# Two empty steps at the end of an mLSTM part: the next part begins two ticks later

## Chip, core and metric

One core of a Trainium2 chip runs the whole program. The metric is device time in microseconds (us), the median of several executions. A core has five instruction queues that run beside each other and wait for each other by semaphores: TensorE (PE; its weight loads are shown as PEld), VectorE (DVE), ScalarE (ACT), GpSimd (POOL) and SyncE (SP), which here issues the DMAs.

## What is computed

One layer of a hybrid decoder block on 2048 positions of width 1024, float32. The part that matters here, cut from the reference:

```python
mod = c_act @ w_ada[l] + b_ada[l]
sh1, sc1, gt1, sh2, sc2, gt2 = [m[:, None, :] for m in jnp.split(mod, 6, axis=-1)]
h = rms_norm(x, g_mix[l]) * (1.0 + sc1) + sh1
p = h @ w_in                      # q_a k_a v_a | q_m k_m v_m o_m | u_s v_s | gates
y_attn = forgetting_attention(qa, ka, va, fa)          # 8 heads of 64
hm = mlstm_chunkwise(qm, km, vm, im, fm)               # 4 heads of 64
y_mlstm = jax.nn.sigmoid(o_m) * rms_norm(hm, g_m_out)
y_sgu = spatial_gating(gelu(u_s), gelu(v_s), g_sgu, w_s, b_s)
x = x + gt1 * (jnp.concatenate([y_attn, y_mlstm, y_sgu], -1) @ w_out)
x = x + gt2 * conv_ffn(rms_norm(x, g_ffn[l]) * (1.0 + sc2) + sh2, ...)
```

The mLSTM carries a state from one chunk of positions to the next, so its chunks are done in order.

## The kernel before

The program has a projection stage (h @ w_in with the mLSTM, the spatial gating and the preparation of the attention's q, k and v), then attention, the output projection, and the feed-forward network. The change is in the projection stage.

Every large product is made of three passes on split operands (a high and a low part): `mm3`, lines 54 to 56. The positions are taken in two halves of 1024. For each half seven blocks of columns are projected, in the list `blocks`: km with the gates, q/o of the mLSTM, vm, the gating's u and v (`use_sgu`), then the attention's k, q and v. A block has eight products of 24 large matmuls (8 steps of k, three passes each); `products` runs one of them. The result of a product stands in one of three PSUM buffers `acc` until VectorE and ScalarE have read it.

From the second block of a half to its sixth, every engine's order is as written (`manual_schedule`), and it is made by ticks. `tick` is called at the end of each product, and in blocks of 512 columns also in the middle of it, after twelve large matmuls. A tick does three things: it may advance a chore by one step (`rest_of_mod`, the remaining modulation vectors, whose accumulation on VectorE, lines 480 to 488, is summed over partitions on PE two ticks later: line 502 for columns, copied out by lines 505 and 507, or line 496 for a gate row, copied out by line 498); it runs what `after(n, f)` has put off until now (`due`); and it advances the first generator in the list `background` by one step, to its next `yield`. Only when that generator has ended is it taken off the list, and the next one begins at the following tick.

The generators are `rows(qi)`, which prepares the gates, and `mlstm(qi)`, a part of 512 positions in four chunks of 128. `mlstm(0)` and `mlstm(1)` belong to the first half, `mlstm(2)` and `mlstm(3)` to the second; the second of each pair stands behind the first in `background`. A part does, in order: loads of two chunks (lines 962 to 970); three empty steps; `turned(0)`, the transposes of kn (line 978, copied to kT by ScalarE, line 980); `decay(0)` (matmuls 952 and 953, exponentials 956) with `turned(1)`; then for each chunk a step with the scores and the state's share (1001, 1003, read by VectorE in 1004, 1005), a step with the values and the state's update (1018, 1022, read in 1019, 1031; the load of the chunk after next is issued here), and a step with the next decay. At its end stands the normalisation of all four chunks (1044 to 1057, on VectorE, ScalarE and GpSimd), two empty steps, one more multiply (1060), and two transposes back, put off by several ticks by `after` (`leave`: 1066 on PE, 1068 on VectorE, 1069 the write).

Beside it, at their own ticks: line 750 mixes positions for the gating, 759 transposes its result (761 copies it on ScalarE); 783 to 791 normalise a product for k or q, and 799 transposes it one and a half products later (803 on ScalarE, 804 on VectorE, 806 the writes to k_d or q_d). `wr` (line 599) are the next block's weights, cast by lines 609 and 610.

Four PSUM names are shared. `mp` has one buffer: lines 502, 496 and 978 write it. `mps` has two: 952, 1001, 1003, 1018, 1022 and 1066 take them in turn. `trp` has two: 750, 759, 799.

Of the kernel before, what the change touches and what calls it, by code (L numbers as in the profile page):

```python
# [33 lines left out]
def trunk(  # L34
# [356 lines left out]
    def mps():  # L391
        return pp.tile([P, 512], F32, name="mps", tag="mps")
# [257 lines left out]
    def natural(half, wb, consume):  # L650
        wide[0] = wb.width == 512
        for i in range(8):
            tt = half * 8 + i
            tb, o = tt // 4, (tt % 4) * P
            ps = acc_ps()

            def mm(k):
                hh, hl = hT[tb, k]
                mm3(ps[:, : wb.width], hh[:, o : o + P], hl[:, o : o + P], *wb.tiles[k], k == 0, k == KT - 1)

            products(i, mm)
            consume(tt, ps)

    def after(n, f):

        pending.append((ticks[0] + n, f))
# [37 lines left out]
    def use_vm(tt, ps):  # L704
        t = pool.tile([P, 256], F32, name="ev", tag="ev")
        V.tensor_copy(t, ps[:, 0:256])
        dma(vm_d[tt * P : (tt + 1) * P, :], t)
        if tt % 8 == 3:
            background.append(mlstm(tt // 4))
# [230 lines left out]
    def mlstm(qi):  # L940
# [122 lines left out]
        def leave(j):  # L1063
            yp = mps()
            for n in range(4):
                T.transpose(yp[:, n * P : (n + 1) * P], hq2[:, n, j * P : (j + 1) * P], ident)
            yt = pool.tile([P, 512], F32, name="yt", tag=("ra", "rb")[j])
            V.scalar_tensor_tensor(yt, yp, gmo[:, j : j + 1], om[:, j, :], op0=ALU.mult, op1=ALU.mult)
            dma(yt_d[512 + j * P : 640 + j * P, t0 : t0 + 512], yt)

        for j in range(2):
            after(6 + j if qi % 2 == 0 else 4 + j, lambda j=j: leave(j))

    nat = lambda use: lambda h, w: natural(h, w, use)
    blocks = [
# [18 lines left out]
    for n, (half, i) in enumerate(steps):  # L1094
# [34 lines left out]
        if i == 2:  # L1129
            background.append(mlstm(half * 2 + 1))  # L1130
# [666 lines left out]
```

## Time and profile before

| | us |
|---|---|
| median of 3 runs | 2602.79 |
| the runs | 2603.23, 2602.79, 2601.43 |
| the profiled execution, its own time | 2602.01 |
| its span, first to last instruction | 2600.3 |

The mean granted clock of TensorE was 0.998 of full speed. mlstm(1) begins its loads at 208.8 us and sends its last write at 299.96; mlstm(3) sends its last at 631.93.

How to read the rows: a row of the time line gives the start in us, the duration in us, the engine, the line of the program, the operation, what it writes and reads, its size, how many instructions of the kind were merged, and in brackets how long the engine stood idle ahead of it and what ended that. A row of waits gives who waited for whom: us in total, times, longest. SPq and PEq are queues ahead of an engine. A row on a tile gives the durations in ns (least, median, most) and the first and last start in us.

### The profile page before, as it was taken

What the parts mean: (1) busy time and instruction counts of PE and PEld (TensorE: products, weight loads), DVE (VectorE), ACT (ScalarE), POOL (GpSimd) and SP (SyncE); (2) the same over time, 40 slices, a digit from 0 to 9 for tenths busy, and PEclk for the clock granted to TensorE, in tenths of its full rate; (3) what the DMA queues carried; (4) which work ended last, traced back from release to release, by engine and by line L of the source; (5) the groups of instructions that cost most, each with busy time, mean ns of one, the idle gap of its engine ahead of it and who ended that gap; (6) DMA issues with size and microseconds to landing.
All of it is one profiled execution on the core that took longest, in us unless ns stands there. A gap on an engine that the chain in (4) does not pass through costs nothing.

```text
span 2600.3 us, 36330 instructions
## 1 busy us (share of the span) xinstructions
PE 2531.4 (97%) x12521; PEld 2094.4 (81%) x12537; DVE 2010.0 (77%) x3433; ACT 1270.3 (49%) x2424; POOL 403.9 (16%) x529
## 2 busy tenths in 40 slices
PE   5999999999999999999999999999999999999999
PEld 5888888888777877778877888888888888788787
DVE  7657656476388888865679888888888887898797
ACT  4343343432388878844455444444444444444443
POOL 2013310133266556510000000000000000000000
PEclk9999999999999999999999999999999999999999
DMA  7345762455564445266823222255222218558523
GB/s 249 114 129 150 218 190 88 136 150 147 172 165 125 128 126 167 54 196 233 283 81 98 81 83 80 82 215 178 85 81 85 86 65 283 174 169 293 184 98 118
DMA packets 302593, 379.58 MB, mean 146 GB/s; under 512 B 31935, under 2 KB 194589, under 8 KB 300361
## 3 DMA queue, kind: packets, MB, share of 16 engines
q1 hardware_dynamic: 302408, 377.26, 46.1%
q8 instruction: 99, 1.62, 0.3%
q14 instruction: 86, 0.70, 0.1%
HBM read 276.44 MB, written 100.74 MB: 145 GB/s over the span
## 4 chain that ended last, share of the span: by engine, by line
PE 43%; DVE 4%; DMA 3%; ACT 1%; issue 0%; SPq 0%; POOL 0%; DVEq 0%; ACTq 0%
PE ub L56 10%; PE ub L54 10%; PE ub L55 10%; PE db L55 4%; PE db L56 4%; PE db L54 4%; DMA wd<-in_w_down_dram 1%; DVE wspl L1474 1%; DMA hc_d<-hl 1%; DMA x_d<-x 0%; DVE wspl L1343 0%; DMA act<-act_d 0%; DVE t2w L1454 0%; DVE B L1208 0%; ACT wsph L1342 0%
## 5 line engine op out<-in xcount | busy, mean ns | idle before, releaser
L54 PE MATMUL acc<-wh,hh 128*128 128x512 f32 (+2 forms) x768 | 284.2, 371 | 1.9 <-DVE vhl L777 1.2
L54 PE MATMUL ub<-T,wsph 128*128 128x512 f32 x704 | 275.9, 392 | 6.5 <-ACT wsph L1342 2.4
L55 PE MATMUL ub<-T,wsph 128*128 128x512 f32 x704 | 275.8, 392 | 0.9 <-DVE T L1208 0.7
L56 PE MATMUL ub<-T,wspl 128*128 128x512 f32 x704 | 275.2, 391 | 0.8 <-DVE wspl L1343 0.7
L56 PE MATMUL acc<-wh,hl 128*128 128x512 f32 (+2 forms) x768 | 273.8, 360 | 1.2 <-DVE st L535 0.9
L55 PE MATMUL acc<-wl,hh 128*128 128x512 f32 (+2 forms) x768 | 273.5, 358 | 0.7 <-DVE wl L610 0.7
L55 PE MATMUL db<-wspl,wsph 128*128 128x512 f32 x616 | 241.0, 392 | 4.9 <-DVE wspl L1474 4.8
L56 PE MATMUL db<-wsph,wspl 128*128 128x512 f32 x616 | 239.5, 389 | 0.0
L54 PE MATMUL db<-wsph 128*128 128x512 f32 x616 | 239.5, 389 | 0.0
L1342 ACT CAST wsph<-S 128x512 fp32r<-128x512 f32 x176 | 109.4, 622 | 217.9 <-PE ub L55 156.5
L263 DVE TENSOR_TENSOR plo<-tp,phi 128x512 fp32r<-128x512 f32 (+1 forms) x320 | 186.9, 607 | 31.0 <-ACT phi L262 28.9
L54 PE MATMUL ub<-B,wsph 128*128 128x512 f32 x528 | 205.7, 390 | 0.0
L55 PE MATMUL ub<-B,wsph 128*128 128x512 f32 x528 | 205.4, 389 | 0.0
L56 PE MATMUL ub<-B,wspl 128*128 128x512 f32 x528 | 205.3, 389 | 0.0
L223 ACT ACTIVATE L<-L,nm 128x1024 f32<-128x1024 f32 (+2 forms) x192 | 172.5, 902 | 34.6 <-DVE nm L212 32.8
L259 PE MATMUL tp<-ident,L 128*128 128x128 f32 x1088 | 177.6, 275 | 4.1 <-DVE plo L263 1.5
L262 ACT CAST phi<-tp 128x512 fp32r<-128x512 f32 (+1 forms) x320 | 160.0, 521 | 42.9 <-PE tp L259 41.2
L1473 ACT CAST wsph<-act 128x512 fp32r<-128x512 f32 x132 | 82.3, 623 | 195.1 <-PE db L55 175.7
L206 PE MATMUL sp<-kk,q 128*128 128x512 f32 (+3 forms) x640 | 170.4, 377 | 3.2 <-DVE nm L212 2.2
L228 POOL TENSOR_SCALAR L<-L,rs 128x1024 f32<-128x1024 f32 (+2 forms) x192 | 167.7, 883 | 11.0
L56 PEld LDWEIGHTS acc<-wh,hl 128*128 128x128 f32 x768 | 144.8, 190 | 23.2 <-DVE hl L580 1.9
L54 PEld LDWEIGHTS ub<-T,wsph 128*128 128x128 f32 x704 | 132.8, 189 | 37.4 <-ACT wsph L1342 6.5
(323 smaller groups left out, 5940.3 us busy)
## 6 DMA issues: line engine op xcount, KB each, us to landing
w<-in_w_up_dram SPq DMA_DIRECT2D x88, 512.0 KB
wd<-in_w_down_dram SPq DMA_DIRECT2D x176, 256.0 KB
wa<-in_w_ada_dram SPq DMA_DIRECT2D x96, 256.0 KB
act_d<-yc SPq DMA_DIRECT2D x44, 512.0 KB
act<-act_d SPq DMA_DIRECT2D x44, 512.0 KB
wr<-in_w_in_dram SPq DMA_DIRECT2D x64, 256.0 KB
q<-q_d SPq DMA_DIRECT2D x128, 128.0 KB
hc_d<-hl SPq DMA_DIRECT2D x28, 512.0 KB
```

The costliest lines, as they stand in the source:

```text
L54: T.matmul(ps, lh, rh, start=start, stop=False, skip_group_check=resume)
L55: T.matmul(ps, lh, rl, start=False, stop=False, skip_group_check=resume)
L56: T.matmul(ps, ll, rh, start=False, stop=stop, skip_group_check=resume)
L206: T.matmul(sp[:, b : b + bw], q2[n][:, qs], kk[:, s0 + b : s0 + b + bw], start=n == 0, stop=n == 1 and not last)
L223: A.activation(L[c], L[c], AF.Exp, bias=nm[:, n - 1 : n], scale=-1.0, accum_out=rs[:, c : c + 1])
L228: G.tensor_scalar(t, t, rs[:, 0:1], 1.0, op0=ALU.mult, op1=ALU.mult)
L259: T.transpose(tp[:, i * P : (i + 1) * P], rows[i][j // 8][:, (j % 8) * P : (j % 8 + 1) * P], ident)
L262: A.copy(hi[:, c0:], tp[:, c0:])
L263: V.tensor_tensor(lo[:, c0:], tp[:, c0:], hi[:, c0:].bitcast(F32), op=ALU.subtract)
L1342: A.copy(hi, src)
L1473: A.copy(hi, v)
L1474: V.tensor_tensor(lo, v, hi.bitcast(F32), op=ALU.subtract)
```

## The change

At the end of the generator `mlstm` two empty steps are added, after `leave` has been put off:

```diff
         for j in range(2):
             after(6 + j if qi % 2 == 0 else 4 + j, lambda j=j: leave(j))
+        yield
+        yield
 
     nat = lambda use: lambda h, w: natural(h, w, use)
```

A part that has done its work stays in `background` for two more ticks, so the part behind it begins two ticks later. What `after` has put off keeps its tick; the chores and the products keep theirs. Behind mlstm(1) and mlstm(3) nothing waits in the list when they end. Outside the stretches of mlstm(1) and mlstm(3) the order of every engine is the same as before, and each engine has the same instructions.

The order moves in three places that are spoken of below. First, TensorE in the gating block of the first half, where the modulation sum (502) writes mp. Before, the transposes of kn (978) for mlstm(1) follow it:

```order
L56 MATMUL acc<-wh,hl 128x512
L502 MATMUL mp<-ones,modacc 128x1 x4
L978 MATMUL mp<-ident,kn 128x128 x2
L54 MATMUL acc<-wh,hh 128x512
L55 MATMUL acc<-wl,hh 128x512
```

Now they stand two ticks further on, behind a leaving transpose of mlstm(0) and a mixing product:

```order
L56 MATMUL acc<-wh,hl 128x512
L1066 MATMUL mps<-ident,hq 128x128 x4
L750 MATMUL trp<-sv,wT 128x256 x2
L978 MATMUL mp<-ident,kn 128x128 x2
L54 MATMUL acc<-wh,hh 128x512
```

Between 502 and 978 there are now 24 large matmuls, two mixing products and one group of leaving transposes.

Second, VectorE at the end of mlstm(1), where the sum of a modulation vector (482, 488) for the next 502 is made. Before:

```order
L1055 TENSOR_REDUCE mss<-hq 128x16
L1056 TENSOR_SCALAR mss<-mss 128x16
L785 TENSOR_REDUCE ss<-qsq 128x8
L786 TENSOR_SCALAR ss<-ss 128x8
L482 SCALAR_TENSOR_TENSOR modacc<-wa,cs,modacc 128x512
L791 TENSOR_TENSOR qn<-acc,ss 128x512
L804 SCALAR_TENSOR_TENSOR qlo<-trp,colA,qhi 128x512
L1060 TENSOR_TENSOR hq<-H,mss 128x1024
L785 TENSOR_REDUCE ss<-qsq 128x8
L786 TENSOR_SCALAR ss<-ss 128x8
L482 SCALAR_TENSOR_TENSOR modacc<-wa,cs,modacc 128x512
L488 TENSOR_TENSOR modacc<-modacc,brow 1x512
```

Now:

```order
L1055 TENSOR_REDUCE mss<-hq 128x16
L1056 TENSOR_SCALAR mss<-mss 128x16
L785 TENSOR_REDUCE ss<-qsq 128x8
L786 TENSOR_SCALAR ss<-ss 128x8
L482 SCALAR_TENSOR_TENSOR modacc<-wa,cs,modacc 128x512
L488 TENSOR_TENSOR modacc<-modacc,brow 1x512
L791 TENSOR_TENSOR qn<-acc,ss 128x512
L804 SCALAR_TENSOR_TENSOR qlo<-trp,colA,qhi 128x512
L1060 TENSOR_TENSOR hq<-H,mss 128x1024
```

The normalisation has come one product closer to 488, which now stands ahead of the multiply qn (791) and of 1060.

Third, TensorE in the second half, where the gate row (496) writes mp. Before, it stands ahead of a decay:

```order
L56 MATMUL acc<-wh,hl 128x512
L759 MATMUL trp<-ident,sy 128x128 x4
L496 MATMUL mp<-modacc,ones 128x512
L952 LDWEIGHTS selb
L952 MATMUL mps<-neb_290,selb 128x128
```

Now:

```order
L56 MATMUL acc<-wh,hl 128x512
L759 MATMUL trp<-ident,sy 128x128 x4
L496 MATMUL mp<-modacc,ones 128x512
L1001 MATMUL mps<-qz_295,kT 128x256 x2
L1003 MATMUL mps<-Cst,qT 128x130 x2
```

The gate row keeps its tick, and the part's first scores (1001, 1003) have come to it; the transposes of the second kn (978) for chunk 1 stand twelve large matmuls ahead of it.

## The prediction

> **What bounds the kernel now.** I read the page's first part, then a table of stretches, then who makes TensorE wait in the two stretches that the change touches.
>
> ```profile
> span 2600.3 us, 36330 instructions
> PE 2531.4 (97%) x12521; PEld 2094.4 (81%) x12537; DVE 2010.0 (77%) x3433; ACT 1270.3 (49%) x2424; POOL 403.9 (16%) x529
> 80.00:120.00 40.00, 40.00 (x187) 33.10 (x187) 28.08 (x52) 11.44 (x22) 0.00 (x0) 1.00 0.36 103
> 216.10:219.60 3.50, 1.22 (x10) 1.06 (x10) 2.16 (x8) 0.00 (x0) 1.54 (x2) 1.00 0.94 298
> ```
>
> TensorE (PE) is busy 97% of the span. The third and fourth rows are stretches: length, then busy time of PE, PEld, DVE, ACT and POOL, granted clock, DMA share and GB/s. From 80 to 120 us PE has no gap at all; from 216.10 to 219.60 it works 1.22 us of 3.50. So PE's own work sets the time, and what another order can change is only the gaps. Those gaps, by what ended them (total us, times, longest), in the first half's stretch from 190 to 320 us (four rows) and the second half's from 540 to 660 (three rows):
>
> ```profile
> PE mp L978 <- DVE sh L505: 2.3, 1, 2.3
> PE mp L502 <- DVE modacc L488: 0.5, 1, 0.5
> PE acc L55 <- DVE wl L610: 0.3, 1, 0.3
> PE trp L799 <- DVE qn L791: 0.2, 1, 0.2
> ...
> PE mps L1003 <- DVE yt L1068: 0.4, 1, 0.4
> PE acc L55 <- DVE wl L610: 0.4, 1, 0.4
> PE trp L799 <- DVE qn L791: 0.2, 1, 0.2
> ```
>
> All of them together are 4.3 us. That is the most this change could win here, and one wait is more than half of it.
>
> The Trainium skill, "Perfetto Trace Analysis", section "Identifying the Most-Contended Engine", says that matmul busy time is not a good measure for TensorE and that weight-load busy time should be used. By it the 81% of PEld would leave a fifth of the span as headroom, in which 2.3 us could vanish: that would be a time of about 2602.8. The trace differs: in the stretch without any gap PEld stands at 33.10 of 40 us, 83%, so 81% is already nearly all that this mix of instructions can show.
>
> **The change part by part.** It adds no instruction on a compute engine. mlstm(0) and mlstm(2) stay in the background queue for two ticks longer, so the whole of mlstm(1) and mlstm(3), with its loads, comes two ticks later. A tick here is half a product: twelve matmuls, from 219.70 to 222.54, 2.84 us; so the parts move by some 5.7 us of PE work.
>
> *The large wait.* Rows of the time line:
>
> ```profile
> 216.17 1.05 PE L502 MATMUL mp<-ones,modacc 128*128 128x1 f32 x8
> 217.76 0.43 DVE L737 TENSOR_TENSOR sv<-ev,mu 128x256 f32<-128x256 f32 x1 [1.12 <-POOL mu L128]
> 218.11 0.68 DVE L785 TENSOR_REDUCE ss<-qsq 128x8 f32<-128x512 f32 x1
> 219.30 0.15 DVE L505 COPY sh<-mp 128x4 f32<-128x4 f32 x1
> 219.50 0.44 PE L978 MATMUL mp<-ident,kn 128*128 128x128 f32 x2 [2.29 <-DVE sh L505]
> 219.70 0.48 PE L54 MATMUL acc<-wh,hh 128*128 128x512 f32 x1
> 222.31 0.39 PE L56 MATMUL acc<-wh,hl 128*128 128x512 f32 x1
> 222.54 1.02 PE L750 MATMUL trp<-sv,wT 128*128 128x256 f32 x4
> ```
>
> The modulation sum (L502) writes the one buffer mp; VectorE empties it (L505) only after what stands ahead in its queue, which itself waited for GpSimd; the transposes of kn (L978) want the same buffer and follow at once. In PE's queue nothing may pass them, so the twelve products behind stand still too. In the new order 24 large matmuls (about 5.7 us) and three small groups lie between the two, while L505 was ready 3.1 us after L502 began (219.30 against 216.17). The wait is gone: 2.29 us. Is something late next? VectorE's L505 no longer releases anyone soon; the next mixing products (L750 at 222.54) come 2.3 us earlier and need sv, written by 218.2. They fit.
>
> *The end of a part.* The normalisation of mlstm(1) now falls one product later, directly ahead of the next modulation sum:
>
> ```profile
> 274.35 0.60 PE L799 MATMUL trp<-ident,qn 128*128 128x128 f32 x4
> 276.38 0.17 DVE L1044 TENSOR_SCALAR nd<-H 128x16 f32<-128x16 f32 x1
> 280.28 0.60 PE L799 MATMUL trp<-ident,qn 128*128 128x128 f32 x4
> 280.98 0.68 DVE L785 TENSOR_REDUCE ss<-qsq 128x8 f32<-128x512 f32 x1
> 281.77 0.75 DVE L482 SCALAR_TENSOR_TENSOR modacc<-wa,cs,modacc 128x512 f32<-128x512 f32 x1
> 285.68 0.69 DVE L791 TENSOR_TENSOR qn<-acc,ss 128x512 f32<-128x512 f32 x1 [3.16 <-POOL ss L128]
> 289.65 0.68 DVE L488 TENSOR_TENSOR modacc<-modacc,brow 1x512 f32<-1x512 f32 x1
> 290.38 1.05 PE L502 MATMUL mp<-ones,modacc 128*128 128x1 f32 x8 [0.47 <-DVE modacc L488]
> ```
>
> Before, the sum (L488) stood behind qn, which waited 3.16 us for GpSimd, and PE then waited 0.47. Now L488 stands ahead of that qn. On the old clock: the chain began 2.03 us after the transposes at 274.35 and would begin 2.03 after those at 280.28, at 282.31. From its start to L785 were 4.60 us, to L482 another 0.79, then 0.75 and 0.68: L488 ends at 289.13. PE wants it at 290.38 less 0.47, 289.91. The margin is 0.78, so the wait goes: 0.47 us. If the chain ran 0.78 late, nothing would be won here, and every further us is a loss. The small wait of L799 on qn (0.2) I let stand: its cause, the chain ahead of qn, only moves.
>
> *Second half.* Two terms:
>
> ```profile
> 558.98 0.71 PE L1003 MATMUL mps<-Cst,qT 128*128 128x130 f32 x4 [0.38 <-DVE yt L1068]
> ...
> 482.29 0.44 PE L978 MATMUL mp<-ident,kn 128*128 128x128 f32 x2 [1.14 <-ACT kT L980]
> ...
> 220.37 1.28 ACT L956 ACT_TABLE_LOAD   x1
> 224.04 1.14 ACT L956 ACTIVATE M<-mps,acol 128x128 f32<-128x128 f32 x4 [2.38 <-PE trp L750]
> 225.05 0.39 ACT L980 COPY kT<-mp 128x256 f32<-128x256 f32 x1
> 232.61 0.60 PE L799 MATMUL trp<-ident,qn 128*128 128x128 f32 x4
> 233.25 0.69 ACT L803 ACTIVATE qhi<-trp,colA 128x512 fp32r<-128x512 f32 x1 [7.31 <-PE trp L799]
> ```
>
> L1003 waited 0.38 us because the leaving transposes of mlstm(2) held one of the two mps buffers; they now come a whole half product ahead of the next user of that buffer: 0.38 won. A new neighbour: the gate product L496, which also writes mp, now follows the transposes of kn by only twelve matmuls. With E as the product's end: leaving transposes 0.43 (232.18 to 232.61), L799 0.44 (to 233.05), the decay matmuls 0.44, kn's transposes 0.38, twelve matmuls 2.84, L759 0.44 make L496 wanted at E+4.97. ScalarE starts qhi 0.64 after L799, at E+1.07, and then needs 0.69, table 1.28, M 1.14 and kT 0.39: E+4.57. It fits by 0.4 us. Bounds: 0, and 1.14, the one wait of this kind (L978 behind kT at 482.29). I take 0.2, near the lower end, since the sum fits.
>
> *The DMAs.* Each part's twenty loads (kn, qT, two qz and v for four chunks) sit on SP's queue and move too. mlstm(1)'s third load now stands behind two k_d writes that wait for ScalarE and VectorE:
>
> ```profile
> L962 SPq DMA_DIRECT2D kn<-km_d x16: 326/469/974, 136.5 to 575.7; - x16
> L1010 POOL TENSOR_TENSOR kw<-kn,ecol x16: 607/611/615, 139.5 to 595.5; 128x256 f32<-128x256 f32 x16
> SPq L762 <- ACT evq L761: 8.7, 2, 7.3
> 241.24 0.60 PE L799 MATMUL trp<-ident,qn 128*128 128x128 f32 x4
> 244.43 0.97 SPq L962 DMA_DIRECT2D kn<-km_d  x1
> ```
>
> Behind such writes kn was issued 3.2 us after L799 (241.24 to 244.43), and the first kn landed within 3.0 us (136.5 to the multiply that waited for it at 139.5). In the new order L799 of the next product runs at E+9.55 (E+4.97, then 1.3 for L1001 and L1003, 2.84, 0.44), so kn is there at E+15.75. Its transposes come at E+19.36 (0.44 more, 1.45 for L1018 and L1022, 2.84, the decay 0.45, 2.84, L799 0.44, 1.35). Cover 3.6 us: it costs nothing, and beyond that PE stalls us for us. The x loads that reuse tiles of a part slip by a product as well; they are needed only in the next half's first block.
>
> **Sum.** 2.29 + 0.47 + 0.38 - 0.2 = 2.94 us less. The profiled execution took 2602.01 us (span 2600.3 and 1.7 around it), so 2599.07. The median of the three runs is 2602.79, 0.78 above it: predicted 2599.9.
>
> **The rivals.**
> 1. *Absorbed*: PE arrives 2.3 us earlier at a wait that was hidden, in the k block or later; VectorE is busy 77% of the span. For: all seven waits above are for VectorE. Against: VectorE stood idle itself in the rows above (1.12 and 3.16 us, for GpSimd), so it can follow an earlier PE. Time 2602.8, up to 2603.9 with the full 1.14.
> 2. *Slower*: SP's queue is held before the third load of a part. A write there has waited 7.3 us (L762 row). Held so long, kn is late by 7.3 less the cover of 3.6, 3.7 us, in both halves 7.4; less 2.94 it is 4.5 us more: 2607.3. It turns to a loss when the hold exceeds 3.6 + 1.5 us. Against: the writes ahead of this load wait for copies that ScalarE starts 0.64 us after the transposes.
> 3. *More*: every gap of both stretches closes, 4.3 us: 2598.5, and with the run to run spread (2601.43 to 2603.23) 2597.6.
> 4. *Not what it says*: the two ticks fall where the queue is empty. Against: the order of PE's queue does move, at exactly the wait. 2602.8.
>
> **How the numbers follow.** Forecast 0.64, absorbed 0.18, slower 0.08, more 0.07, nothing 0.03. The likeliest by itself spans 2598.5 to 2601.3. The range takes in 'more' and 'absorbed': 2597.5 to 2603.9. A change of 0.2% is 5.2 us, about what a measurement of this kernel can tell from none: faster means below 2597.6, slower above 2608.0. The forecast's own spread barely reaches the first; from 'more' I take 0.08 for faster, from 'slower' 0.05, and 0.87 remains.
>
> **What would show it.** Right: no row of L978 waiting for L505; PE without a gap between L502 and L750 near 216; no wait of L502 on L488 near 288; no wait of L1003 on L1068; the rest of the kernel starting some 2.5 to 3 us earlier. Wrong: L496 or L978 waiting for kT or for kn, L502's wait grown, or gaps of PE elsewhere that grew by what was won.

## The result and the profile after

| | before | after |
|---|---|---|
| median, us | 2602.82 | 2596.41 |
| lowest and highest run | 2600.35, 2607.48 | 2594.83, 2602.30 |
| the profiled execution | 2602.01 | 2596.29 |
| its span | 2600.3 | 2594.6 |

The ratio of after to before is 0.9979, 95% interval [0.9972, 0.9986]: 5.5 us less, between 3.6 and 7.3. (The two medians of the table differ by 6.4, inside that interval; what is compared from here on is the ratio with its interval.) The sign and the places were as predicted, the size was not: 2.9 us had been forecast, and 2596.4 lies 1.1 us below the low end of the range.

The first part of the page after: span, then busy time of each engine.

```profile
span 2594.6 us, 36323 instructions
PE 2530.4 (98%) x12521; PEld 2095.3 (81%) x12537; DVE 2010.4 (77%) x3433; ACT 1270.5 (49%) x2424; POOL 403.0 (16%) x529
```

PE's busy time is 2531.4 before and 2530.4 now, with the same number of matmuls; the span fell by 5.7. The work did not shrink. Who makes PE wait in the changed kernel, first in the stretch from 190 to 320 us, then from 535 to 660:

```profile
PE acc L55 <- DVE wl L610: 0.3, 1, 0.3
...
PE acc L55 <- DVE wl L610: 0.4, 1, 0.4
```

These two rows are all that is left of seven in this profile. The time line of the changed kernel, PE where the large gap was, PE at the next modulation sum, and VectorE ahead of that sum:

```profile
216.48 1.05 PE L502 MATMUL mp<-ones,modacc 128*128 128x1 f32 x8
217.39 0.48 PE L54 MATMUL acc<-wh,hh 128*128 128x512 f32 x1
...
220.23 1.02 PE L750 MATMUL trp<-sv,wT 128*128 128x256 f32 x4
...
223.86 0.60 PE L1066 MATMUL mps<-ident,hq 128*128 128x128 f32 x4
224.29 1.03 PE L750 MATMUL trp<-sv,wT 128*128 128x256 f32 x4
225.16 0.38 PE L978 MATMUL mp<-ident,kn 128*128 128x128 f32 x2
...
287.15 0.39 PE L56 MATMUL acc<-wh,hl 128*128 128x512 f32 x1
287.38 0.95 PE L502 MATMUL mp<-ones,modacc 128*128 128x1 f32 x8
...
280.28 0.17 DVE L1044 TENSOR_SCALAR nd<-H 128x16 f32<-128x16 f32 x1
284.88 0.68 DVE L785 TENSOR_REDUCE ss<-qsq 128x8 f32<-128x512 f32 x1
286.45 0.68 DVE L488 TENSOR_TENSOR modacc<-modacc,brow 1x512 f32<-1x512 f32 x1
```

The products follow L502 after 0.91 us (216.48 to 217.39) where they took 3.53 before, and L978 stands 8.7 us behind L502, with no idle time ahead of it. L488 ends at 287.13 and L502 starts at 287.38, 0.23 behind the last product, the distance of one product from the next.

A measure of the first half follows from two rows, the first transposes of the gating's result (L759) and the first transposes of the second half's normalised x (L574). They stand outside the moved part, and the work of PE between them is the same in both orders. A measure of the second half is made in the same way, from its own first L759 to the first matmul of the attention (L206):

```profile
203.93 0.60 PE L759 MATMUL trp<-ident,sy 128*128 128x128 f32 x4
...
367.51 1.03 PE L574 MATMUL trp<-ident,xt 128*128 128x128 f32 x8
...
532.89 0.60 PE L759 MATMUL trp<-ident,sy 128*128 128x128 f32 x4
...
666.51 0.62 PE L206 MATMUL sp<-kk,q 128*128 128x512 f32 x2
```

For the kernel before, the same four rows:

```profile
203.59 0.60 PE L759 MATMUL trp<-ident,sy 128*128 128x128 f32 x4
...
370.56 1.03 PE L574 MATMUL trp<-ident,xt 128*128 128x128 f32 x8
...
536.48 0.60 PE L759 MATMUL trp<-ident,sy 128*128 128x128 f32 x4
...
670.89 0.61 PE L206 MATMUL sp<-kk,q 128*128 128x512 f32 x2
```

The first half takes 163.6 us after and 167.0 before: 3.4 won, where the forecast had 2.76. The second takes 133.6 after and 134.4 before: 0.8 won, where the forecast had 0.18. These lengths, "the first half" and "the second half" from here on, are the finest rulers in the case. The total is a coarse one: executions of the same program spread over some 8 us.

### The profile page after: what moved, and what is told of

The parts are those of the page before. It is cut to its first block, busy times and chain, and to the rows that moved or that the text cites. A ratio compares the mean times of both kernels' runs of the same rounds, so it can differ in the third digit from the quotient of the medians.

```text
span 2594.6 us, 36323 instructions
## 1 busy us (share of the span) xinstructions
PE 2530.4 (98%) x12521; PEld 2095.3 (81%) x12537; DVE 2010.4 (77%) x3433; ACT 1270.5 (49%) x2424; POOL 403.0 (16%) x529
## 4 chain that ended last, share of the span: by engine, by line
PE 43%; DVE 4%; DMA 3%; ACT 1%; issue 0%; SPq 0%; POOL 0%; DVEq 0%; ACTq 0%
PE ub L56 10%; PE ub L55 10%; PE ub L54 10%; PE db L55 4%; PE db L56 4%; PE db L54 4%; DMA wd<-in_w_down_dram 2%; DVE wspl L1476 1%; DMA hc_d<-hl 1%; DMA x_d<-x 0%; DVE wspl L1345 0%; DMA act<-act_d 0%; DVE t2w L1456 0%; DVE B L1210 0%; DVE T L1210 0%
## 5 line engine op out<-in xcount | busy, mean ns | idle before, releaser
L55 PE MATMUL ub<-T,wsph 128*128 128x512 f32 x704 | 275.8, 392 | 0.9 <-DVE T L1210 0.7
L55 PE MATMUL acc<-wl,hh 128*128 128x512 f32 (+2 forms) x768 | 274.1, 359 | 0.7 <-DVE wl L610 0.7
L55 PE MATMUL db<-wspl,wsph 128*128 128x512 f32 x616 | 241.1, 392 | 5.3 <-DVE wspl L1476 5.0
L55 PE MATMUL ub<-B,wsph 128*128 128x512 f32 x528 | 205.4, 389 | 0.0
L206 PE MATMUL sp<-kk,q 128*128 128x512 f32 (+3 forms) x640 | 169.4, 375 | 3.3 <-DVE nm L212 2.2
L228 POOL TENSOR_SCALAR L<-L,rs 128x1024 f32<-128x1024 f32 (+2 forms) x192 | 167.7, 883 | 11.0
```

What stands on the lines that cost most here:

```text
L55: T.matmul(ps, lh, rl, start=False, stop=False, skip_group_check=resume)
L206: T.matmul(sp[:, b : b + bw], q2[n][:, qs], kk[:, s0 + b : s0 + b + bw], start=n == 0, stop=n == 1 and not last)
L228: G.tensor_scalar(t, t, rs[:, 0:1], 1.0, op0=ALU.mult, op1=ALU.mult)
```

## The experiments

The letters in an expectation are those of its own text. From the fifth run on they are: A, a closed gap is worth its own length; G, the gap of 2.29 us also lowers PE's granted clock behind it.

| run | median us | ratio to before, 95% interval | first half us | clock below 1 at 216 to 224 us |
|---|---|---|---|---|
| profile of before | 2602.82 | 1 | 167.0 | no |
| after | 2596.41 | 0.9979 [0.9972, 0.9986] | 163.6 | no |
| e1_control | 2602.04 | 1.0003 [0.9994, 1.0012] | 168.4 | yes |
| e2_first | 2596.72 | 0.9982 [0.9973, 0.9990] | 163.6 | no |
| e3_second | 2599.84 | 0.9997 [0.9988, 1.0006] | 168.4 | yes |
| e4_both | 2595.11 | 0.9979 [0.9970, 0.9988] | 163.6 | no |
| e5_mp | 2597.22 | 0.9984 [0.9975, 0.9992] | 164.5 | no |
| e6_fill | 2603.60 | 1.0009 [1.0000, 1.0018] | 167.1 | no |
| e7_one | 2596.56 | 0.9980 [0.9971, 0.9989] | 163.5 | no |
| e8_putback | 2600.72 | 0.9998 [0.9989, 1.0007] | 167.7 | yes |
| e9_fill2 | 2603.27 | 1.0006 [0.9996, 1.0015] | 167.0 | no |
| e10_backfill | 2599.15 | 0.9992 [0.9983, 1.0000] | 166.2 | no |
| e11_fill_next | 2599.30 | 0.9990 [0.9981, 0.9999] | 163.6 | no |
| e12 to e15, single runs | 2602.59, 2598.50, 2595.54, 2604.33 | | 168.3, 167.1, 167.1, 168.6 | yes, no, no, yes |

Each row's before is that of its own chip session.

### One half at a time

The empty steps stand under a condition. In e2_first it is `qi == 0`, in e3_second `qi == 2`, and e4_both has none, which is the change itself. For the control, e1_control, it is the one below: the steps stand where the list is empty anyway, so that its order is that of before (the edit against before):

```diff
+        if qi % 2 == 1:
+            yield
+            yield
```

> The two empty steps stand only at the end of mlstm(1) and mlstm(3), behind which nothing waits: every engine's instructions and order are those of the kernel before. All theories: the time of before, ratio 1.000. What it tells is how far two executions of one program differ, and whether the wait of 1.14 us of L978 on kT near 482 us, seen in the one profile of before, is there each time (theory A: it hangs on when a w_in transfer lands and comes and goes; theory B: it belongs to the old order and will be there again).

> The two empty steps only after mlstm(0), so only mlstm(1) begins later. Theory A (the sum of the closed TensorE gaps): 2.29 + 0.47 + 0.15 = 2.9 us less, 2599.9. Theory C (an earlier TensorE also wins later, in attention and in the output projection, about as much again): 4.5 to 6 us less.

> The two empty steps only after mlstm(2), so only mlstm(3) begins later. Theory A: 0.38 + 0.16 = 0.5 us less, 2602.3. Theory B (the 1.14 near 482 us is closed by the change in the first half): no more than 0.5 here either. If the whole change gives 6 us and the first half alone 3, then this must give 2 to 3, and the closed gaps are not the account.

> The changed kernel once more, on the same chip as the halves: 5.5 to 6.4 us less than before if the first result stands; 3 us if it was the chip. The halves should add up to it (theory A: 2.9 + 0.5 = 3.4).

Most of the gain lies in the first half: 0.9982 there, 0.9997 in the second, and both together 0.9979, which is their product. By the total the second half cannot be told from nothing; its ruler tells it: 134.36 to 134.43 us in each of the ten profiles with the old order there, 133.46 to 133.65 in each of the seven with mlstm(3) moved. Theory C for the first half (4.5 to 6 us) is not told from A (2.9) by the interval of 2.6 to 7.0. But no later gain shows where C looked for it: from the first L206 to the feed-forward network's first product it is 636.8 to 641.0 us in the seven profiles with the old first half, and 637.8 to 640.5 in those of after, e2, e4 and e7. The rows of waits went where the parts of the edit were: the first half's edit left L1003's 0.4, the second's left L978's 2.3.

The control has the program of before, and its total is not told from that of before, but its time line behind the gap reads otherwise:

```profile
219.54 0.69 PE L978 MATMUL mp<-ident,kn 128*128 128x128 f32 x2 [2.28 <-DVE sh L505]
219.88 0.78 PE L54 MATMUL acc<-wh,hh 128*128 128x512 f32 x1
220.46 0.63 PE L55 MATMUL acc<-wl,hh 128*128 128x512 f32 x1
220.88 0.63 PE L56 MATMUL acc<-wh,hl 128*128 128x512 f32 x1
...
222.16 0.52 PE L56 MATMUL acc<-wh,hl 128*128 128x512 f32 x1
222.52 0.39 PE L54 MATMUL acc<-wh,hh 128*128 128x512 f32 x1
...
223.90 1.02 PE L750 MATMUL trp<-sv,wT 128*128 128x256 f32 x4
```

The products start 0.43 us apart instead of 0.23 until 222.5, and L750 comes 4.36 us after L978; in the profile of before, which the prediction quotes, it came 3.04 after it. So the gap had a second price here, some 1.3 us, and the one profile of before happened not to show it. The granted clock, the third column from the right, from 220 to 224 us, in before and then in the control:

```profile
220.00:224.00 4.00, 3.95 (x23) 3.26 (x22) 1.49 (x3) 1.64 (x2) 0.87 (x1) 1.00 0.11 39
```

```profile
220.00:224.00 4.00, 4.00 (x15) 3.23 (x14) 0.69 (x1) 1.66 (x2) 0.91 (x1) 0.70 0.09 33
```

PE's busy time is as high in the control, 4.00 of 4, with 15 matmuls in place of 23: a table of busy shares alone does not show the loss.

### The wait alone, taken away and put back

In e5_mp, made from before, the kn transposes ahead of mlstm(1) write mps:

```diff
-            kps = misc_ps()
+            kps = mps() if (qi, n) == (1, 0) else misc_ps()
```

> The order of before, except that the transposes of kn (L978) ahead of mlstm(1) write one of the two mps buffers instead of mp, so that they no longer wait for L505. Theory A (a closed gap is worth its own length): 2.3 us less than before, ratio 0.9991, the waits of 0.5 and 0.4 stay. Theory G (the gap of 2.29 us also takes the granted clock down behind it, by about 1.4 us, in two of three executions): 3.2 to 3.8 us less, ratio 0.9986 to 0.9988, granted clock 1.00 from 216 to 224 us. Rival: the wait moves on to the buffers of mps, 0.

The order is that of before, with only the buffer changed. L978 no longer waits:

```profile
217.79 1.05 PE L502 MATMUL mp<-ones,modacc 128*128 128x1 f32 x8
218.70 0.42 PE L978 MATMUL mps<-ident,kn 128*128 128x128 f32 x2
218.87 0.48 PE L54 MATMUL acc<-wh,hh 128*128 128x512 f32 x1
```

From L502 to the first product it is 1.08 us instead of 3.53: 2.45 won, and the first half is 2.5 shorter than that of before (no drop of the clock in either). This one wait is the larger part of the change: 0.9984 against 0.9979 in total, 2.5 of 3.4 us in the first half. The interval allows 2.1 to 6.5 us, so the total does not separate A (2.3) from G (3.2 to 3.8).

In e8_putback, made from after, two transposes behind L502 write mp, and nothing reads them:

```diff
                 V.tensor_copy(sh2[:, sl], ps[:, 0:4])
+                if half == 1:
+                    again = misc_ps()
+                    for j in range(2):
+                        T.transpose(again[:, j * P : (j + 1) * P], ident, ident)
```

> The changed order, but right behind L502 of this vector's halves two transposes into mp whose result nothing reads, so that TensorE waits for L505 again where it did before. Theory A: the 2.3 us come back and all the rest of the gain stays, so about 3.2 us less than before, ratio 0.9988. Theory G: 2.3 and 1.4 come back, 1.5 to 2 us less than before, ratio 0.9993, and the granted clock below 1 from 216 to 224 in some profiles. A third theory, that the gain comes from the later place of the part and not from this wait: 5 us less, ratio 0.998.

With the later part kept and the wait put back, the total is no longer told from that of before: 0.9998. Its rows (L509 is the added pair of transposes):

```profile
221.45 0.69 PE L509 MATMUL mp<-ident 128*128 128x128 f32 x2 [2.31 <-DVE sh L505]
221.79 0.78 PE L54 MATMUL acc<-wh,hh 128*128 128x512 f32 x1
222.36 0.63 PE L55 MATMUL acc<-wl,hh 128*128 128x512 f32 x1
```

The first half is 167.7, 4.1 more than with the change: 2.3 for the wait, some 1.3 for the products at the lower clock, and the rest the two transposes and the restart. The third theory, that the gain lies in the part's later place as such, expected 0.998 and falls. A's 0.9988 lies just outside the interval, G's 0.9993 inside.

### The gap filled

In e6_fill, made from before, matmuls that nothing reads stand ahead of the kn transposes:

```diff
             if (qi, n) == (1, 0):
+                fill = mps()
+                for _ in range(8):
+                    T.matmul(fill, identb, maskT.rearrange("p h t -> p (h t)"), start=True, stop=True)
```

> The order of before; TensorE does 8 additional small matmuls into an unused mps buffer between L502 and L978, which nothing reads, while L978 still waits for L505. Theory A: the gap is filled but the products start no earlier, 0 us, ratio 1.000, or a little more time. Theory G: the products behind the gap run at the full clock, 0.9 to 1.4 us less, ratio 0.9995 to 0.9997, with granted clock 1.00 from 220 to 224 us and the rows of L54 to L56 at about 0.23 us apart from the first on.

```profile
217.08 1.05 PE L502 MATMUL mp<-ones,modacc 128*128 128x1 f32 x8
217.99 1.89 PE L979 MATMUL mps<-maskT,identb 128*128 128x512 bf16 x8
220.42 0.44 PE L982 MATMUL mp<-ident,kn 128*128 128x128 f32 x2 [0.54 <-DVE sh L505]
220.62 0.48 PE L54 MATMUL acc<-wh,hh 128*128 128x512 f32 x1
```

The products start 3.54 us behind L502, as in before, and at the full clock: first half 167.1, 1.3 below the control. That much is as G says. But the total did not follow: 1.0009, where G expected 0.9995 to 0.9997. Two more runs asked why. In e9_fill2, made from before, the eight fall on both buffers (the edit's two lines that differ from e6; the matmul stands under them):

```diff
+                for fill in (mps(), mps()):
+                    for _ in range(4):
```

> As the run with the gap filled, but the 8 additional matmuls stand in both mps buffers, 4 in each, so that who gets which of the two buffers later in the program is as before. Theory G (a gap of 2.29 us brings a lowered clock behind it in most executions): granted clock 1.00 from 216 to 224 us, first half from the first L759 to the first L574 about 167.0 us as in the profile of before without the drop, and 0.5 to 1.4 us less than before in total, ratio 0.9995 to 0.9998. Rival, the swapped buffers made the former run longer: this one is below it by 2 us. Rival, the drops of the clock are displaced to other places of the program rather than removed: ratio 1.000 or above again, with the first half at 167.0.

In e10_backfill the same stands in e8_putback, ahead of its two transposes (cut in the same way):

```diff
+                    for fill in (mps(), mps()):
+                        for _ in range(4):
```

> The changed order with the wait at mp put back (two transposes whose result nothing reads) and the gap filled by 8 additional matmuls into both mps buffers. Theory G: granted clock 1.00 from 216 to 226 us; first half 166.3, 1.4 less than the 167.7 with the wait put back and nothing in the gap; in total 0.9 to 1.4 us less than that run, ratio to before 0.9993 to 0.9995. Theory A: the same as that run, 0.9998.

In e9 the buffers are taken by the others as before, and the time is the same as in e6: the swapped buffers were not the reason. In e10 the filling did what G says, 166.2 against 167.7 in the first half and 0.9992 against 0.9998 in total, but these two intervals overlap. In the three profiles with the gap filled, the clock was lowered a little later, behind the wait of L574 at the start of the second half, which is 1.8 us in the changed kernel and was 1.9 (e6, e10) and 3.1 us (e9) in these three. This is that stretch in e6 and in e10:

```profile
375.00:380.00 5.00, 5.00 (x31) 4.99 (x30) 4.93 (x10) 4.29 (x8) 0.00 (x0) 0.66 0.66 204
```

```profile
375.00:380.00 5.00, 5.00 (x35) 5.00 (x34) 4.20 (x10) 4.05 (x7) 0.00 (x0) 0.74 0.57 179
```

The others show a lowered clock there in three of fourteen. This fits a drop that is displaced rather than removed, but three profiles are few. The granted clock on record for all eleven executions does not decide it: its mean is 0.9968 in e6 and 0.9970 in e9, beside 0.9966 and 0.9964 for before on the same chips. It does say that no lower clock kept these totals up. Why they did not fall stays open.

### The size of the move, and the next gap

In e7_one, made from after:

```diff
         yield
-        yield
```

> One empty step in place of two. The transposes of kn have moved away from L502 already, by half a product. Theory A: 2.3 us less for the gap at L978, the 0.5 of L502 perhaps left, together 2.3 to 2.9, ratio 0.9989 to 0.9991. Theory G: about 3.7 to 4.5, ratio 0.9983 to 0.9986, clock 1.00 from 216 to 224.

One empty step does what two do: 0.9980, the same rows of waits, the first half 163.5 and the second 133.5. Half a product between L502 and L978 is enough.

In e11_fill_next, made from after, the filling stands behind the second group of transposes of the second half's x (L574), where PE waits 1.8 us in the changed kernel:

```diff
             for i in range(4):
                 T.transpose(ps[:, i * P : (i + 1) * P], xs[i][:, k * P : (k + 1) * P], ident)
+            if (tb, k) == (2, 1):
+                for fill in (mps(), mps()):
+                    for _ in range(4):
+                        T.matmul(fill, identb, maskT.rearrange("p h t -> p (h t)"), start=True, stop=True)
```

> The changed kernel, and in the next gap of that size, 1.8 us at about 368 us where the first transposes of the second half's normalised x (L574) wait for ScalarE, 8 additional matmuls that nothing reads; the order of the products just behind moves a little with it. If what the clock lost there in four of ten profiles can be won by filling, 0.5 to 1 us less than the change, ratio to before 0.9976; if filling only displaces the drops, the same as the change, 0.998.

The stretch from 365 to 380 us ran at the full clock in its profile. But PE still waited 0.8 us for ScalarE, and 1.2 for VectorE at 383 us, where the longest such wait in the profile after is 0.45, and the total, 0.9990, is not below the change. No version here beats the change.

### How often the clock drops

> The program of before once more (the empty steps where no part ends), one profile. Asked: how often the granted clock is below 1 between 216 and 224 us. Theory G: in two of three profiles; then the first half (first L759 to first L574) takes 168.4 us, else 167.0. If the drop is rare, 167.0.

> The same, a second profile: 168.4 with the drop, 167.0 without.

> The same, a third profile: 168.4 with the drop, 167.0 without.

> The same, a fourth profile: 168.4 with the drop, 167.0 without. With the three profiles of the old order so far, in which the drop stood in two, theory G expects four or five of seven in all; a rare drop two of seven.

All four have the gap of 2.29 us; the drop came in two. Over the old order with the gap unfilled (before, e1, e3, e12 to e15) it is four of seven: first half 168.3 to 168.6 with it, 167.0 or 167.1 without. With e8 it is five of eight profiles with the gap, and none of nine without it or with it filled.

What goes with it can be read from the traces, which record when the clock was lowered and for how long. In all 17 profiles every lowered stretch, but for one at the very end of the program, lasts 3.41 us or twice that, at a granted clock of 0.50. Within a profile these stretches begin a whole number of steps of 3.413 us apart: in the control at 44.93, 219.01 and 1335.17 us, which is 51 and 327 steps. So the clock changes on a grid that is fixed within one execution and lies differently in the next. The control's two steps around the gap, and then the step of before whose start falls into the gap:

```profile
215.60:219.01 3.41, 1.66 (x11) 1.17 (x10) 2.22 (x7) 0.00 (x0) 1.01 (x2) 1.00 0.95 280
219.01:222.42 3.41, 2.88 (x8) 2.41 (x9) 1.17 (x4) 1.66 (x2) 1.80 (x1) 0.50 0.37 142
```

```profile
217.68:221.09 3.41, 1.58 (x8) 1.37 (x9) 1.83 (x6) 1.09 (x2) 1.85 (x2) 1.00 0.74 252
```

In the five profiles with the drop a step of the grid begins 1.65 to 2.29 us after PE fell idle; in the three without it, 0.38 to 0.44 us after (worked out from their later drops). This parts all eight. Where between 0.44 and 1.65 us the limit lies, no run shows.

The time of a run does not hang on this place alone: e15 (2604.33) has drops at 220, 680, 1025 and 1335 us, e14 (2595.54) of these only the last. The same gap of 1.24 us near 680, in e12 and then in e14, PE's row and the stretch:

```profile
680.35 0.79 PE L54 MATMUL acc<-wh,hh 128*128 128x512 f32 x1 [1.24 <-DVE vhl L777]
...
680.00:685.00 5.00, 4.65 (x11) 3.68 (x12) 1.15 (x3) 1.41 (x5) 4.80 (x9) 0.50 0.86 279
```

```profile
680.43 0.50 PE L54 MATMUL acc<-wh,hh 128*128 128x512 f32 x1 [1.24 <-DVE vhl L777]
...
680.00:685.00 5.00, 4.57 (x20) 3.82 (x21) 1.22 (x5) 1.48 (x6) 4.80 (x9) 1.00 0.84 282
```

The same program, the same wait, and the matmul behind it takes 0.79 or 0.50 us. The 1.24 us were not the whole reason: in e12 the lowered stretch begins at 679.65, in the middle of that wait, and in the 3.41 us ahead of it PE was busy 2.04, broken by shorter waits.

## Why the prediction was right in kind and wrong in size

*What bounds the kernel* held in one half: PE's work did not change, gaps did. That "what another order can change is only the gaps" did not hold: behind a gap the same matmuls can take longer. *Each closed wait* was named rightly: L978 behind L505, L502 behind L488, L1003 behind L1068 have no row after.

*The large wait* is the step that failed: "The wait is gone: 2.29 us." Its mechanism is shown by taking the wait away (e5) and putting it back (e8). Its size was taken from the row of the wait alone. The runs showed 2.45 for the restart of the products (3.53 less 1.08 in e5), and behind it products at a lower clock in four of seven profiles, 1.3 to 1.6 us of the first half each time, 0.8 on the mean (4/7 of 1.4). The stretch behind the gap had a granted clock of 1.00 in the only profile that I had, and I took that for a property of the kernel. The ceiling fell with this step: "All of them together are 4.3 us. That is the most this change could win here" prices every gap at its length. (L505 starts 3.13 us after L502 and has ended after 3.28; I called it ready at its start, which changes nothing here.)

The Trainium skill, "TensorE: Matmul & The Clock Gate", Part 1, says that the gate watches a free-running window of about 3.4 us, that it halves the clock after an idle one, and that for this reason the slow matmuls at the start of one kernel differ in number from run to run. The runs agree on the step of 3.41 us, on the half and on the change from run to run, and show the same in the middle of a program. They differ on how idle a window must be: in the five profiles PE was busy 1.1 to 1.8 of the 3.41 us ahead of the drop, and in e12 near 680 us 2.04.

*The end of a part*: I had the chain start 2.03 us after the transposes and 0.78 us of margin left. In the new order it starts 2.03 us after them again (278.25 to 280.28), and the sum L488 ended in time, by 0.25 us (287.13 against 287.38). The 0.47 went, with no idle time of L502. L799's wait in the first half, which I "let stand", has no row after either; it is missing in e1 and e14 too, whose order is the old one, so it is not the change's alone. The step from e5 to the change, 164.5 to 163.6, is 0.9 us for L502 and L799, where their rows say 0.63 at most.

*Second half*: L1003's 0.38 went, and the 0.2 that I charged for L496 behind kT did not come: neither L496 nor L978 has a row of waiting. L799's 0.16 is not part of it: it is still there in e3 and e4, where mlstm(3) moved, and missing in e14, where it did not. The ruler says 0.8 won, twice the row of L1003; the rows do not show where the rest comes from. The wait of 1.14 us at 482 us, my upper bound for L496, comes and goes with the execution: 0.2 in the control, 0.9 in e9, no row in e12 to e15.

*The sum* then reads: first half 3.4 (167.0 to 163.6), clock 0.8, second half 0.8 (134.4 to 133.6), together 5.0 us, for a measured 5.5 (3.6 to 7.3). The last 0.5 lies within that interval and has no measured term. The share of the clock is the least certain one. The granted clock on record for every execution allows more: its mean is 0.9979 in the 11 of e4_both and 0.9965 in the 33 of before beside them, and 0.0014 of 2600 us is 3.6 us, an upper bound, since a lowered clock costs nothing while PE stands idle. In e5 the same working gives 0.8 (0.9969 against 0.9966). What weakens it: filling the gap in the old order (e6, e9) gave the clock back inside the first half, and the total did not fall.

*The rivals*: "absorbed" and "not what it says" fell at once: L574 starts 3.1 us earlier (367.51 against 370.56), and in the two stretches no new wait took the place of the old ones. "Slower" fell: the loads of mlstm(1) made PE wait nowhere. "More" was nearest, but for a wrong reason: it summed the rows of all gaps to 4.3 us, and two of these rows, L55 behind wl (0.3 and 0.4), are still there. The range ended at that sum, as if a gap could cost no more than its length.

## What to carry to other kernels

A gap of PE can cost more than its row of waiting: look at the starts of the matmuls behind it and at the granted clock there, in more than one profile of the same program, before pricing it. Where one buffer is written twice in close succession on the engine that bounds the kernel, half a product of other work between the two writers can do what a second buffer does (here e7, 0.9980, and e5, 0.9984). A total that spreads over 8 us is read together with a local ruler between two rows that the edit does not move.

## What was not expected of the hardware

The clock drop after short gaps is not fixed by the program: behind 2.29 us it came in five of eight profiles, by where a grid of 3.41 us lay against the gap, and near 680 us, around a wait of 1.24, in one of the two shown and not in the other. It lasts 3.41 us in the control, from 219.01 to 222.42; the large matmuls in it start 0.43 us apart instead of 0.23, and the busy share hides it. The profiles show such drops near 45, 220, 375, 680, 1020, 1120 and 1330 to 1350 us, each in some of them, and at the very end in all. e14, the shortest of the four single runs, has fewer of them than e15, the longest. Over the 93 executions of before beside the experiments a longer time goes with a lower granted clock, but loosely (correlation -0.50, -0.60 and -0.25 in the three sessions), so that the drops are a part of the spread of 8 us between executions of one program and not the whole of it. That filling one gap left the total where it was remains open.
